# Where the second weight block of a VectorE sum is loaded: a change in the buffers of a feed-forward product

## The chip, the cores and the metric

The kernel runs on one core of a Trainium2 chip, as one program. The metric is the device time of one execution in microseconds; the time before is the median of three runs, 956.37 us (955.89 to 956.82). A profiled execution is recorded beside them, from which all rows below are taken.

## The reference

The kernel computes one layer of a hybrid decoder on 1040 rows (16 learned rows and 1024 of input) of 1024 columns: an input projection, sliding-window attention beside a gated linear recurrence, an output projection, and then a feed-forward part. The change lies in the feed-forward part, whose reference is

```
u = rmsnorm(h, g_pre_ffn[l])
f = jnp.square(jax.nn.relu(u @ w_ff1[l])) @ w_ff2[l]
h = h + rmsnorm(f, g_post_ffn[l])
```

`w_ff1` is 1024 x 4096, `w_ff2` is 4096 x 1024, all in float32.

## The kernel before

All large products are made on TensorE from float32 operands that are split in two: a high half (a cast to the rounded format, made by ScalarE at L96) and a low half (the operand less its high half, made by VectorE at L99). A product is then three matmuls: high by high (L125), high by low (L130) and low by high (L131).

Both feed-forward products are cut in two by two blocks, and made with seven block products instead of eight (Strassen's scheme). The second, `f`, is the last part of the program, from about 606 us on. `PLAN` lists its seven products `i` = 0 to 6: which blocks of the activation are added (`fx`), which blocks of `w_ff2` are added or subtracted (`wx`), and into which output quarters the product goes. Each product runs over eight slices `q` of the contracted dimension, so that there are 56 steps, numbered n = 8i + q. A step is 24 matmuls: four row tiles of 128, each with two sub-slices and three matmuls, each into its own PSUM bank.

For a step the weight sum has to be formed, cast and split. Its blocks are 128 x 1024 floats, 512 KB each:

- `fetch_2(n)` (L1258) loads the blocks. The first goes to a buffer by a load of SP's queue (L1270). The second, where the blocks are added, either is added to the first in the buffer by an accumulating transfer of GpSimd's queue (L1267, slices with `q % 3 < 2`), or is loaded to a second buffer by SP (L1270, in the slices 2 and 5).
- `prep_2(n)` (L1274) adds two blocks on VectorE where there are two (`combine`, L997: the sum goes to the first buffer), then makes the high half (ScalarE) and the low half (VectorE) into a pair of `ws` buffers, and does the same for the activation, into `b` buffers.

Steps whose sums are made by VectorE in the products 1 and 2 are (1, 2), (1, 5), (2, 2) and (2, 5), that is n = 10, 13, 18 and 21. The products 3 and 4 subtract, and take two loads in every step. The product 0 and 5 have a single block.

Buffers come from named kinds ("tags"), each with a fixed number of buffers of 4 KB or a little more in each partition. `raw` and `e` have two each, `d` has four, `ws` five, of which one holds `g_post_ffn` in this part, so that a step's pair comes free when TensorE has ended the step two before it. In the second part three of the four `d` buffers hold activations. The fourth is used in the last product by `finish_half(3)` (L1364), which loads the last rows of the residual stream for the end of the kernel (used at L1408).

Which blocks are fetched when is a loop over the steps that runs some four steps ahead. The order in which the instructions stand on each engine and in each queue is set by a scheduler at build time, by its own estimate of when buffers come free. Each queue is then worked in order: an instruction that waits holds up all behind it.

Of the kernel before, what the change touches and what calls it, by code (L numbers as in the profile page):

```python
# [37 lines left out]
def hybrid_layer(  # L38
# [19 lines left out]
    def slot(tag, shape, dt=F32):  # L58
        uid[0] += 1
        return slab.tile(shape, dt, tag=tag, name=f"{tag}{uid[0]}", bufs=bufs[tag])  # L60
# [1197 lines left out]
    def fetch_2(n):  # L1258
        i, q = steps[n]
        wx = PLAN[i][1]  # L1260
        tags = (("raw", "e"), ("e", "raw"))[n % 2] if i < 6 else LASTW[q]
        raws = []
        for (a, b), tag in zip(wx[:2], tags):
            if len(wx) == 3 and wx[2] is ADD and raws and (
                q % 3 < 2 if i < 6 else tag is None
            ):
                nc.gpsimd.dma_start(raws[0], w2v[q, a, b], accum_op=ADD)  # L1267
                break
            r = slot(tag, [P, 2, 512])
            nc.sync.dma_start(r, w2v[q, a, b])  # L1270
            raws.append(r)
        return raws
# [32 lines left out]
    for n, p in enumerate(third):  # L1305
        if n + 2 < 16:
            raw_c[third[n + 2]] = fetch_c(third[n + 2])
        if n >= 13:
            raw_2[n - 13] = fetch_2(n - 13)
        if n + 1 < 16:  # L1310
            wc[third[n + 1]] = prep_c(third[n + 1])
        if n == 15:
            gffn_b = slot("ws", [P, D])
            nc.gpsimd.dma_start(gffn_b, g_post_ffn[0].partition_broadcast(P))
            ready[0] = prep_2(0)
        if p not in a12_early:
            y2 = bank(("acc", "s")[p % 2])
            product(y2, wc[p][0], ob21, True)
            nc.vector.tensor_tensor(block("11", p), y2, block("11", p), op=ALU.add)
        y4 = bank(("pt", "o")[p % 2])  # L1320
        if n == 0:
            product_by_parts(y4, wc[p][1], ot4)
        else:
            product(y4, wc[p][1], ot4, True)
        nc.vector.tensor_tensor(block("21", p), y4, block("21", p), op=ALU.add)
        done.add(p)
        if p ^ 1 in done:
            activate("11", p // 2)
            activate("21", p // 2)
# [119 lines left out]
    for n, (i, q) in enumerate(steps):  # L1449
        while fetched < min(n + (4 if n < 45 else 6), len(steps)):  # L1450
            raw_2[fetched] = fetch_2(fetched)
            fetched += 1
        if n + 1 < len(steps):
            late = w_low[0]
            ready[n + 1] = prep_2(n + 1, "a" if n + 1 >= len(steps) - LAST else "ws")
        if q == 0:
            old = None if i == 0 else accs
            accs = [[bank(("acc", "s", "pt", "o")[j])] for j in range(4)]
            if i == 6:

                evict(5, 0, old[0][0], late)
                accs[3] = [accs[3][0][:, :256], bank("acc")[:, :256]]
        if n < len(steps) - LAST:
            for j in range(4):
                for acc, cols in zip(accs[j], col_parts(i, j)):
                    step_mm(acc, j, q, ready[n], cols)
            del ready[n]
        if old and (q > 0 or i < 6) and q < 4:
            evict(i - 1, q, old[q][0], late)
        if (i, q) in EARLY:  # L1470
            finish_early(EARLY.index((i, q)))
        if i == 6 and 1 <= q < 5:
            finish_half(q - 1)
# [36 lines left out]
```

## Time and profile before

| | |
|---|---|
| median of three runs | 956.37 us (955.89 to 956.82) |
| the profiled execution's own time | 954.71 us |
| its span, first to last instruction | 953.0 us |
| TensorE busy | 941.2 us, 99% of the span |
| VectorE, ScalarE, GpSimd busy | 658.9, 507.8, 132.1 us |
| granted clock of TensorE over the span | 0.999 |

The rows of the profile name the engines PE (TensorE), PEld (its weight loads), DVE (VectorE), ACT (ScalarE), POOL (GpSimd) and SP (SyncE); a "q" behind an engine means its queue. A timeline row gives the start in us from the start of the span, the duration, the engine, the line, the operation and the tiles (out<-in, with the buffers' kinds as names), and in brackets how long the engine sat idle before it and what ended that. "To landing" is the time from a transfer's issue until its data is there.

### The profile page before, as it was taken

How to read it: one execution, taken by the hardware profiler on the slowest of the kernel's cores; microseconds unless marked ns; L12 is line 12 of the kernel's file. 1: busy time of each engine (PE TensorE's matmuls, PEld its weight loads, DVE VectorE, ACT ScalarE, POOL GpSimd, SP SyncE). 2: the span in 40 equal slices, each digit the busy share in tenths (PEclk: the TensorE clock that was granted, in tenths of full speed). 3: DMA queues.
4: the chain of work that ended last, by engine and by line, in shares of the span. 5: the costliest groups of instructions: out<-in, count | busy, mean ns of one | idle time of the engine just before them, and what ended most of it. 6: DMA issues, size and time to landing. Idle time of an engine off the chain costs nothing.

```text
span 953.0 us, 12421 instructions
## 1 busy us (share of the span) xinstructions
PE 941.2 (99%) x4712; PEld 787.1 (83%) x4712; DVE 658.9 (69%) x849; ACT 507.8 (53%) x858; POOL 132.1 (14%) x205
## 2 busy tenths in 40 slices
PE   9999999999999999999999999999999999999997
PEld 8999999877888878888888888888888788888885
DVE  6668788879865887665644465476568576769883
ACT  8546766568645564443655575654433343445441
POOL 4104546410020100010000000001111100001201
PEclk9999999999999999999999999999999999999999
DMA  8220011104225468674422364334778765637934
GB/s 272 56 67 23 24 45 44 46 23 133 86 108 174 142 220 266 199 239 151 163 89 88 111 201 131 101 114 117 175 171 202 180 199 178 198 134 201 241 66 89
DMA packets 88199, 130.21 MB, mean 137 GB/s; under 512 B 13702, under 2 KB 52630, under 8 KB 88140
## 3 DMA queue, kind: packets, MB, share of 16 engines
q1 hardware_dynamic: 78972, 104.44, 34.4%
q0 software_dynamic: 8880, 24.19, 11.9%
q8 instruction: 37, 0.61, 0.3%
q10 hardware_dynamic: 288, 0.79, 0.2%
q14 instruction: 22, 0.18, 0.1%
HBM read 109.93 MB, written 18.87 MB: 135 GB/s over the span
## 4 chain that ended last, share of the span: by engine, by line
PE 91%; DVE 5%; ACT 2%; issue 1%; DMA 0%; DVEq 0%; SPq 0%
PE ps_acc L125 10%; PE ps_acc L131 10%; PE ps_acc L130 10%; PE ps_s L131 6%; PE ps_s L130 6%; PE ps_s L125 6%; PE ps_pt L130 6%; PE ps_pt L131 6%; PE ps_pt L125 6%; PE ps_o L131 5%; PE ps_o L130 5%; PE ps_o L125 5%; ACT c L82 1%; PE ps_o L696 1%; PE ps_acc L282 1%
## 5 line engine op out<-in xcount | busy, mean ns | idle before, releaser
L99 DVE TENSOR_TENSOR ws<-raw,ws 128x1024 fp32r<-128x1024 f32 (+1 forms) x69 | 82.6, 1197 | 71.0 <-ACT ws L96 24.1
L96 ACT CAST ws<-raw 128x1024 fp32r<-128x1024 f32 (+1 forms) x68 | 69.7, 1025 | 92.8 <-PE ps_o L130 25.0
L125 PE MATMUL ps_acc<-a,ws 128*128 128x256 f32 (+2 forms) x272 | 88.6, 326 | 0.7 <-DVE b L479 0.4
L130 PE MATMUL ps_acc<-a,ws 128*128 128x256 f32 (+2 forms) x272 | 87.9, 323 | 0.0
L96 ACT CAST ws<-e 128x1024 fp32r<-128x1024 f32 x41 | 43.0, 1050 | 83.4 <-PE ps_o L130 33.2
L131 PE MATMUL ps_acc<-a,ws 128*128 128x256 f32 (+2 forms) x272 | 87.5, 322 | 0.0
L99 DVE TENSOR_TENSOR b<-b,b 128x1024 fp32r<-128x1024 f32 (+2 forms) x50 | 58.9, 1178 | 24.7 <-PE ps_o L130 19.5
L99 DVE TENSOR_TENSOR ws<-e,ws 128x1024 fp32r<-128x1024 f32 x41 | 50.1, 1222 | 33.4 <-ACT ws L96 20.0
L96 ACT CAST b<-b 128x1024 fp32r<-128x1024 f32 (+2 forms) x49 | 50.0, 1019 | 43.6 <-DVE b L997 38.1
L683 POOL TENSOR_SCALAR_AFFINE_SELECT c<-c 128x512 fp32r<-128x512 f32 x64 | 55.5, 884 | 68.9 <-ACT c L96 54.9
L125 PEld LDWEIGHTS ps_acc<-a,ws 128*128 128x128 f32 x272 | 51.3, 188 | 5.4 <-issue 0.9
L131 PEld LDWEIGHTS ps_acc<-a,ws 128*128 128x128 f32 x272 | 51.2, 188 | 4.0 <-issue 0.2
L130 PEld LDWEIGHTS ps_acc<-a,ws 128*128 128x128 f32 x272 | 51.2, 188 | 3.7 <-issue 0.2
L125 PE MATMUL ps_acc<-ws,b 128*128 128x512 f32 (+1 forms) x120 | 46.4, 388 | 1.1 <-ACT ws L96 1.1
L130 PE MATMUL ps_acc<-ws,b 128*128 128x512 f32 (+1 forms) x120 | 46.2, 385 | 0.1
L131 PE MATMUL ps_acc<-ws,b 128*128 128x512 f32 (+1 forms) x120 | 46.2, 385 | 0.0
L125 PE MATMUL ps_pt<-ws,b 128*128 128x512 f32 x112 | 44.2, 395 | 0.0
L131 PE MATMUL ps_pt<-ws,b 128*128 128x512 f32 x112 | 44.1, 394 | 0.0
L130 PE MATMUL ps_pt<-ws,b 128*128 128x512 f32 x112 | 44.1, 393 | 0.0
L125 PE MATMUL ps_s<-ws,b 128*128 128x512 f32 x110 | 43.5, 395 | 0.0
L130 PE MATMUL ps_s<-ws,b 128*128 128x512 f32 x110 | 43.4, 394 | 0.0
L131 PE MATMUL ps_s<-ws,b 128*128 128x512 f32 x110 | 43.2, 393 | 0.0
(413 smaller groups left out, 2660.0 us busy)
## 6 DMA issues: line engine op xcount, KB each, us to landing
raw<-in_w_ff_dram SPq DMA_DIRECT2D x61, 512.0 KB, 3.5
e<-in_w_ff_dram SPq DMA_DIRECT2D x45, 512.0 KB, 4.0
a<-in_w_ff_dram SPq DMA_DIRECT2D x12, 512.0 KB, 5.5
s_dram<-a POOLq DMA_DIRECT2D x12, 512.0 KB, 3.8
raw<-in_w_in_dram SPq DMA_DIRECT2D x9, 512.0 KB, 3.8
c<-in_x_dram SPq DMA_DIRECT2D x8, 512.0 KB, 4.9
d<-in_x_dram SPq DMA_DIRECT2D x8, 512.0 KB, 4.6
out_dram<-raw SPq DMA_DIRECT2D x8, 512.0 KB
```

The source lines that it names most:

```text
L82: ins = nc.scalar.activation(*args, **kwargs).ins
L96: nc.scalar.copy(hi, src)
L99: low = nc.vector.tensor_tensor(lo, src, f32(hi), op=ALU.subtract).ins
L125: ins = nc.tensor.matmul(dst, lh, rh, start=start, stop=False, skip_group_check=True).ins
L130: nc.tensor.matmul(dst, lh, rl, start=False, stop=False, skip_group_check=True)
L131: last_mm[0] = nc.tensor.matmul(dst, ll, rh, start=False, stop=stop, skip_group_check=True).ins.name
L282: last_mm[0] = nc.tensor.matmul(acc[:, :n], w[k // 2][:, kc, :], u[kc][k % 2][:, t0 : t0 + n], start=k == 0 and kc == 0, stop=k == last an ...
L683: nc.gpsimd.affine_select(out=p_[:, :, s], in_=f32(p_[:, :, 0]), pattern=[[0, 4], [g, P]], compare_op=op, fill=0.0, base=0, channel_multip ...
L696: nc.tensor.matmul(two[:, :, oc : oc + w], v, p_.rearrange("p (j i) s c -> p j (i s c)", j=2)[:, :, pc : pc + w], start=n == 0 and k == 0, ...
```

## The change

In the steps of the products 1 and 2, the second of the two buffers is taken from the kind `d` instead of `raw` or `e`. Steps whose second block is added by the accumulating transfer take no second buffer, so only the steps 10, 13, 18 and 21 are touched.

```
         tags = (("raw", "e"), ("e", "raw"))[n % 2] if i < 6 else LASTW[q]
+        if i in (1, 2):
+            tags = tags[0], "d"
         raws = []
         for (a, b), tag in zip(wx[:2], tags):
```

The order of the built program changes with it. On TensorE and ScalarE it stays. On VectorE the sums of the steps 10, 13 and 18 move one to three places ahead, to before the low half of an earlier step; the sum of step 21 stays. On GpSimd's queue the accumulating transfers of the steps 22 and 23 change places, so that 22 comes first. On SP's queue the second blocks of the steps 10, 13, 18 and 21 come earlier: that of step 10 stands where the load of `finish_half(3)` stood, in the third part of the first feed-forward product; those of 13, 18 and 21 stand ahead of the first blocks of the steps 11, 14 and 19. The load of `finish_half(3)` stands behind the first block of step 23. The first block of step 22 stands ahead of that of step 23.

More of the change, by code (lines that the diff above doesn't have):

```diff
@@ L1261, in fetch_2 @@
         tags = (("raw", "e"), ("e", "raw"))[n % 2] if i < 6 else LASTW[q]
+        if i in (1, 2):
+            tags = tags[0], "d"
         raws = []
```

## The prediction

> **What bounds the kernel now.** I read the page first, then what TensorE waits for, then the timeline of every engine around that wait. A step is called by its number n = 8i + q (product i, block q): the four steps of the change are 10, 13, 18 and 21.
>
> ```profile
> PE 941.2 (99%) x4712; PEld 787.1 (83%) x4712; DVE 658.9 (69%) x849; ACT 507.8 (53%) x858; POOL 132.1 (14%) x205
> ...
> PE 91%; DVE 5%; ACT 2%; issue 1%; DMA 0%; DVEq 0%; SPq 0%
> ```
>
> TensorE is busy for 941.2 of 953.0 us, and the chain that ended last runs 91% over it. The number of its instructions does not change, so the change can only give or take TensorE's idle time. Of that there is one piece in the whole second feed-forward part. The waits of TensorE from 600 to 945 us show it:
>
> ```profile
> PE ps_acc L125 <- ACT ws L96: 1.1, 1, 1.1
> ```
>
> Its place, in the timeline of TensorE:
>
> ```profile
> 754.42 0.40 PE L131 MATMUL ps_o<-ws,b 128*128 128x512 f32 x1
> 755.91 0.50 PE L125 MATMUL ps_acc<-ws,b 128*128 128x512 f32 x1 [1.09 <-ACT ws L96]
> 756.25 0.39 PE L125 MATMUL ps_s<-ws,b 128*128 128x512 f32 x1
> 756.48 0.40 PE L125 MATMUL ps_pt<-ws,b 128*128 128x512 f32 x1
> 756.72 0.40 PE L125 MATMUL ps_o<-ws,b 128*128 128x512 f32 x1
> 757.17 0.50 PE L130 MATMUL ps_acc<-ws,b 128*128 128x512 f32 x1
> 757.51 0.39 PE L131 MATMUL ps_acc<-ws,b 128*128 128x512 f32 x1
> ```
>
> Starts follow each other by 0.23 us here (756.25 to 756.48). Beyond that pitch, 754.42 to 755.91 loses 1.26, 755.91 to 756.25 loses 0.11, 756.72 to 757.17 loses 0.22 and 757.17 to 757.51 loses 0.11: 1.70 us together. The boundary is that between steps 21 and 22. A step is 24 matmuls, 24 x 0.23 = 5.5 us.
>
> What was late is step 22's high half, a cast on ScalarE:
>
> ```profile
> 743.46 1.05 ACT L96 CAST ws<-e 128x1024 fp32r<-128x1024 f32 x1 [1.91 <-PE ps_o L130]
> ...
> 754.82 1.04 ACT L96 CAST ws<-raw 128x1024 fp32r<-128x1024 f32 x1 [7.79 <-PE ps_o L131]
> ```
>
> The cast at 743.46 is step 21's. Its buffer came free when TensorE ended step 19, so step 22's was due one step later, at 749.0. The row names TensorE for the 754.82, but the ws buffers that step 22 takes are those of step 20, done by 749.0. What else the cast needs is its weight sum, which POOL's queue makes by an accumulating transfer:
>
> ```profile
> 732.11 1.22 POOL L1267 DMA_DIRECT2D raw<-in_w_ff_dram  x1 [6.75 <-issue]
> 740.95 1.20 POOL L1267 DMA_DIRECT2D e<-in_w_ff_dram  x1 [7.62 <-DVE b L997]
> 748.76 1.22 POOL L1267 DMA_DIRECT2D raw<-in_w_ff_dram  x1 [6.61 <-issue]
> ```
>
> ```profile
> DMA to landing us min/median/max: 6.0/6.7/7.5
> ```
>
> The second fence is L1267's between 739 and 756 us, that is of the last two rows: 7.5 and 6.0 us. The one of 740.95 (into e, step 23) landed at about 748.45, and only 0.3 us later the one of 748.76 (into raw, step 22) went out. It landed at 748.76 + 6.0 = 754.76, just ahead of the cast. So accumulating transfers run one at a time, and step 23's stands before step 22's although it is needed later.
>
> Why step 22 is second is seen in SP's loads and the VectorE work that frees their buffers:
>
> ```profile
> 729.18 1.22 DVE L99 TENSOR_TENSOR ws<-raw,ws 128x1024 fp32r<-128x1024 f32 x1
> ...
> 734.72 1.22 DVE L99 TENSOR_TENSOR ws<-e,ws 128x1024 fp32r<-128x1024 f32 x1
> ...
> 736.46 1.21 DVE L997 TENSOR_TENSOR e<-e,raw 128x1024 f32<-128x1024 f32 x1
> ```
>
> ```profile
> 730.42 0.37 SPq L1270 DMA_DIRECT2D raw<-in_w_ff_dram  x1
> ```
>
> ```profile
> 735.97 0.37 SPq L1270 DMA_DIRECT2D e<-in_w_ff_dram  x1
> 737.70 0.37 SPq L1270 DMA_DIRECT2D raw<-in_w_ff_dram  x1
> ```
>
> Step 18's low half ends at 730.40 and frees a raw buffer, but step 21's second block takes it (730.42). Step 22's first block gets the raw that step 21's sum frees at 736.46 + 1.21 = 737.67 (737.70), after step 23's first block at 735.97.
>
> **The change part by part.** *No work is added.* Four loads of 512 KB, four sums, and all accumulating transfers stay; only buffers and places in the queues of SP, POOL and VectorE move. That costs nothing by itself.
>
> *The first of the four second blocks* (step 10) finds a d buffer free early and stands in SP's queue where the load of the last residual rows stood. That load goes behind step 23's first block and waits for step 21's sum:
>
> ```profile
> L1364 SPq DMA_DIRECT2D d<-out_dram x1: 498/498/498, 540.4 to 540.4; - x1
> ```
>
> ```profile
> L1408 DVE SCALAR_TENSOR_TENSOR a<-a,rs,d x2: 746/749/752, 947.6 to 948.2; 128x512 f32<-128x512 f32 x2
> ```
>
> From about 738 to its use at 947.6 it has 209 us: nothing. The sums of step 10 lose nothing by a block that is there 120 us early.
>
> *The other three second blocks* wait on SP for the sum before them, because one d buffer is turned over. Queued behind them are the loads of steps 11 and 12, of 14, and of 19. Before, the first of each group waited for the same sum too, since that sum freed its raw or e buffer. So SP's queue gets these no later, unless the sum itself is later: the price is nothing, and that of the exception is in the last rival.
>
> *Step 22 on POOL.* Now step 22's first block takes the raw free at 730.40, and on POOL its accumulating transfer stands ahead of step 23's (the built program has them so). The load is there by 730.42 + 5.2 = 735.6 even at the slow rate shown below. The transfer before it on POOL, at 732.11, was over by 740.95 at the latest; at 6.0 it was over by 738.1. Of all L1267 the times are these:
>
> ```profile
> DMA to landing us min/median/max: 5.6/6.0/9.3
> ```
>
> At the median step 22 lands at 738.1 + 0.3 + 6.0 = 744.4, at the worst 741.3 + 9.3 = 750.6; the cast (1.05 us) must be over by 754.65. Cover: 9.2 us, at worst 3.0. Step 23 then lands 6.3 later (750.7), at worst 9.6 later (760.2), and its cast must be over at 754.65 + 5.5 = 760.2: 8.4 us of cover, and at worst 1.0 short, which takes three extreme transfers in a row. The whole 1.70 us goes.
>
> A page of the Trainium skill would see nothing there: DMA: Bandwidth & Descriptors, Anatomy of one DMA, fits about 2.0 us plus bytes over 436 GB/s for a transfer from GpSimd's queue, an estimate of 3.2 us for 512 KB. By that step 22 would have landed at 740.95 + 3.2 + 0.3 + 3.2 = 747.7, ahead of the 749.0, and the sum would be 0. The measured 7.5 and 6.0 decide against it for transfers that also add.
>
> *What is late next.* After step 22 comes step 24's sum, which keeps its time, and then step 25's:
>
> ```profile
> 751.08 1.22 DVE L997 TENSOR_TENSOR raw<-raw,e 128x1024 f32<-128x1024 f32 x1 [0.73 <-DMA e<-in_w_ff_dram]
> ```
>
> ```profile
> 760.72 1.23 DVE L997 TENSOR_TENSOR e<-e,raw 128x1024 f32<-128x1024 f32 x1 [1.33 <-DMA raw<-in_w_ff_dram]
> ```
>
> Step 24's sum leaves step 22's low half, queued behind it on VectorE, ending at 751.08 + 1.22 + 1.22 = 753.5, before the 754.65. Step 25's raw block goes into step 22's buffer and comes earlier with it, by more than the 1.70. So TensorE stays fed, and 1.70 is carried to the end.
>
> *Sum.* The profiled execution took 954.71 us, its span 953.0: 954.71 - 1.70 = 953.0. The median of the runs shown is 956.37, 1.66 above that execution: 956.37 - 1.70 = **954.7**. The bounds of the gain: 1.70 hangs on two transfers of 7.5 + 6.0 = 13.5 us. Two of 5.6 would leave nothing to gain. This one took far longer:
>
> ```profile
> 701.58 1.22 POOL L1267 DMA_DIRECT2D e<-in_w_ff_dram  x1 [5.05 <-DVE b L997]
> ...
> 710.44 1.20 POOL L1267 DMA_DIRECT2D raw<-in_w_ff_dram  x1 [7.64 <-issue]
> ```
>
> 8.9 us from one issue to the next is 8.6 of transfer; with 6.0 behind it the two make 14.6, and the gain 2.8. If all 1.66 by which the runs exceed the profiled execution were this stall, the gain would be 3.4, and the time 953.0.
>
> **The rivals.** *The rows are right by their letter:* ScalarE's cast waited for TensorE, not for the transfer, and the change removes nothing: 956.4. For it speaks the releaser named at 754.82; against it that every other step frees its buffer two steps ahead, and that the landing falls within 0.06 us of the cast. I give it 0.10.
>
> *The sums come too early.* In the built program the sums of steps 10, 13 and 18 stand one to three places earlier on VectorE, ahead of the low halves of steps 7, 10 and 15, which TensorE wants. A sum that waits for its first block holds those up. Issue of the first block, and the casts from which the due times follow:
>
> ```profile
> 662.69 0.37 SPq L1270 DMA_DIRECT2D raw<-in_w_ff_dram  x1
> ```
>
> ```profile
> 680.36 0.37 SPq L1270 DMA_DIRECT2D e<-in_w_ff_dram  x1
> ```
>
> ```profile
> 708.18 0.37 SPq L1270 DMA_DIRECT2D raw<-in_w_ff_dram  x1
> ```
>
> ```profile
> 671.27 1.05 ACT L96 CAST ws<-raw 128x1024 fp32r<-128x1024 f32 x1 [4.53 <-PE ps_o L130]
> ...
> 687.91 1.05 ACT L96 CAST ws<-e 128x1024 fp32r<-128x1024 f32 x1 [1.01 <-PE ps_o L130]
> ...
> 710.20 1.05 ACT L96 CAST ws<-e 128x1024 fp32r<-128x1024 f32 x1 [2.05 <-PE ps_o L130]
> ```
>
> The cast at 671.27 marks the start of step 7, that at 687.91 of step 10, and step 15 starts at 710.20 + 5.5 = 715.7. TensorE first uses low halves after four matmuls, 0.9 later: 672.2, 688.8, 716.6. Sum and low half take 2.4. So the loads may take 672.2 - 2.4 - 662.7 = 7.1, 6.0 and 6.0 us. What they take, beside an accumulating transfer:
>
> ```profile
> 689.85 1.23 DVE L997 TENSOR_TENSOR e<-e,raw 128x1024 f32<-128x1024 f32 x1 [4.07 <-DMA raw<-in_w_ff_dram]
> ```
>
> ```profile
> 684.68 0.37 SPq L1270 DMA_DIRECT2D raw<-in_w_ff_dram  x1
> ```
>
> ```profile
> DMA to landing us min/median/max: 3.2/3.6/7.6
> ```
>
> That load took 5.2 us, under 6.0 by 0.8; the median of L1270 is 3.6, the longest 7.6. At 7.6 the three stalls are 0.5 + 1.6 + 1.6 = 3.7, against the 1.70: +2.0, 958.4. It turns slower above 6.9 us (twice 0.85 over). The loads do move closer to the accumulating transfers, so I give it 0.18. In the Trainium skill, DMA: Bandwidth & Descriptors, Issuing engines are not separate DMA queues, has transfers of all queues share the same 16 engines and interleave, and so speaks against the change in this place; the 5.2 against 3.6 agrees.
>
> **How the numbers follow.** Stall removed 0.72, nothing removed 0.10, sums too early 0.18. The bound of 0.2% is 1.9 us, about what a measurement of this kernel can tell from no change, and 1.70 lies just inside it. Of the 0.72 I put 0.42 beyond (the runs are longer than the profiled execution, and 0.2 us more of stall is enough) and 0.30 within. So faster 0.42, same 0.40, slower 0.18. The range reaches from 953.0 (gain 3.4) to the last rival's 958.4.
>
> **What would show it.** Right: no wait of TensorE on ScalarE near 755; two POOL transfers in a row into raw and e there in that order, raw first, landed before 750; SP's residual load near 738. Wrong: TensorE idle before low halves near 672, 689 or 716 with VectorE's sum just ahead; or the gap at 754.4 unchanged, with the cast starting although the transfer had long landed.

## The result and the profile after

The changed kernel takes 953.29 us (median of seven runs, 953.15 to 953.75), the kernel before 956.37 (seven runs, 954.32 to 958.12). The ratio is 0.9966, with an interval of 0.9953 to 0.9980: faster by 0.34%, or 3.1 us. The runs also lie closer together, 0.6 us from end to end for 3.8. The profiled execution of the changed kernel took 953.59 us, its span 951.9.

TensorE works as long as before (941.2 us), so what is gone is idle time:

```profile
PE 941.2 (99%) x4712; PEld 787.7 (83%) x4712; DVE 659.2 (69%) x849; ACT 508.2 (53%) x858; POOL 131.4 (14%) x205
```

The boundary of the steps 21 and 22 in TensorE's timeline, the place of the 1.70 us:

```profile
754.58 0.40 PE L130 MATMUL ps_o<-ws,b 128*128 128x512 f32 x1
754.82 0.40 PE L131 MATMUL ps_o<-ws,b 128*128 128x512 f32 x1
755.06 0.39 PE L125 MATMUL ps_acc<-ws,b 128*128 128x512 f32 x1
755.29 0.39 PE L125 MATMUL ps_s<-ws,b 128*128 128x512 f32 x1
```

The starts follow each other by 0.23 to 0.24 us straight through. From 600 to 945 us the list of TensorE's waits is empty. Step 22's cast, the second of these rows of ScalarE's timeline, and the accumulating transfers on POOL (two lines were added to the kernel, so that L1267 and L1270 are now L1269 and L1272):

```profile
743.86 1.05 ACT L96 CAST ws<-e 128x1024 fp32r<-128x1024 f32 x1 [1.91 <-PE ps_o L130]
...
749.45 1.06 ACT L96 CAST ws<-raw 128x1024 fp32r<-128x1024 f32 x1 [2.02 <-PE ps_o L130]
...
755.02 1.05 ACT L96 CAST ws<-e 128x1024 fp32r<-128x1024 f32 x1 [3.57 <-PE ps_o L130]
```

```profile
734.96 1.20 POOL L1269 DMA_DIRECT2D raw<-in_w_ff_dram  x1 [6.56 <-DMA raw<-in_w_ff_dram]
742.62 1.22 POOL L1269 DMA_DIRECT2D e<-in_w_ff_dram  x1 [6.47 <-DVE ws L99]
```

Step 22 (raw) now goes out at 734.96 instead of 748.76, ahead of step 23 (e). Its cast starts at 749.45, when its buffer comes free, and no longer at 754.82. The loads on SP in this stretch:

```profile
736.37 0.37 SPq L1272 DMA_DIRECT2D e<-in_w_ff_dram  x1
738.10 0.34 SPq L1366 DMA_DIRECT2D d<-out_dram  x1
```

Step 22's first block is not among them any more (it went out at 730.82). The residual load (into d) stands where the prediction put it.

In the accounts below, the stall of an execution is the sum of what TensorE loses between 600 and 930 us. It is worked out from TensorE's timeline: each distance of two starts above 0.29 us counts, less the pitch of 0.23. Ratios are to the kernel before on the same chip, with a 95% interval in brackets.

### The profile page after: what moved, and what is told of

It is laid out like the page before. It is cut to its first block, busy times and chain, and to the rows that moved or that the text cites. A ratio compares the mean times of both kernels' runs of the same rounds, so it can differ in the third digit from the quotient of the medians.

```text
span 951.9 us, 12417 instructions
## 1 busy us (share of the span) xinstructions
PE 941.2 (99%) x4712; PEld 787.7 (83%) x4712; DVE 659.2 (69%) x849; ACT 508.2 (53%) x858; POOL 131.4 (14%) x205
## 4 chain that ended last, share of the span: by engine, by line
PE 86%; DVE 7%; ACT 3%; issue 2%; DMA 2%; SPq 0%; DVEq 0%; POOL 0%; ACTq 0%
PE ps_acc L125 10%; PE ps_acc L131 10%; PE ps_acc L130 10%; PE ps_s L131 6%; PE ps_s L125 6%; PE ps_s L130 6%; PE ps_pt L130 6%; PE ps_pt L131 6%; PE ps_pt L125 6%; PE ps_o L131 5%; PE ps_o L130 5%; PE ps_o L125 5%; ACT c L82 1%; PE ps_o L696 1%; PE ps_acc L282 1%
```

## The experiments

Theory A: step 22 waited for its accumulating transfer because step 23's stood before it. Theory B: the gain comes from the freed `raw` and `e` buffers, by which all loads are earlier. All four kernels of the first set ran on one chip, beside a kernel before with a median of 956.84 us (29 runs, 953.47 to 958.53).

**Step 21 alone.**

```
-        if i in (1, 2):
+        if n == 21:
             tags = tags[0], "d"
```

(on the changed kernel, as is the next)

> Only step 21 takes its second block into a d buffer; steps 10, 13 and 18 stay as before. The built program then has step 22's accumulating transfer ahead of step 23's, and nothing else of weight is moved. Theory A (the order of steps 22 and 23 on GpSimd's queue is the whole cost): the idle time of TensorE at 754 us is gone, about 953.3 us, all of the 3.1 gained. Theory B (the gain comes from three more free buffers, which make all loads of products 1 and 2 earlier): about a quarter of the gain, 955.6 us, and idle time is left near 754.

Measured: 953.61 us (953.01 to 954.36), ratio 0.9970 (0.9959 to 0.9981). One of the four buffers gives all of the gain that can be told apart. Its profile has no stall near 754, and one of 0.31 us at 722.

**The other three alone.**

```
-        if i in (1, 2):
+        if n in (10, 13, 18):
             tags = tags[0], "d"
```

> Steps 10, 13 and 18 take d buffers, step 21 does not; step 23's accumulating transfer stays ahead of step 22's. Theory A: 956.4 us within the spread of before (954.3 to 958.1), with 1 to 4 us of idle time on TensorE at 754. Theory B: about 954.0 us, three quarters of the gain.

Measured: 954.00 us (952.93 to 954.50), ratio 0.9971 (0.9962 to 0.9981). That is theory B's number: here step 23 still stands ahead of step 22, and the gain came all the same. Of the stall at 755, 0.26 us is left. Theory A as stated fell with it: the order is not the only way to the gain.

**The order alone.**

```
+    adds = {}
...
-                nc.gpsimd.dma_start(raws[0], w2v[q, a, b], accum_op=ADD)
+                adds[n] = nc.gpsimd.dma_start(raws[0], w2v[q, a, b], accum_op=ADD).ins
+                if n == 23:
+                    behind(adds[22].name, adds[23])
```

(on the kernel before; `behind(x, y)` makes y stand behind x)

> All buffers as before, but step 23's accumulating transfer is made to stand behind step 22's on GpSimd's queue. Step 22's load is issued at 737.7 as before and lands by about 741.5, so its accumulating transfer runs from about 742 to 748, step 23's to 754 or 756. Theory A: no idle time at 754, about 953.3 us. Theory B: no gain, 956.4 us.

Measured: 953.21 us (952.78 to 955.08), ratio 0.9969 (0.9959 to 0.9979). All buffers are those of before, and the gain is whole. Theory B as stated fell too. Its profile has no stall at 754, and 0.45 us at 694.7, of which more below.

**All four buffers, with the old order.**

```
...
+                if n == 23:
+                    behind(adds[23].name, adds[22])
```

(on the changed kernel; `adds` is filled as in the edit above)

> All four d buffers as in the changed kernel, but step 22's accumulating transfer is made to stand behind step 23's again. Step 23's load lands at about 741, its accumulating transfer at 748, step 22's at 754. Theory A: the idle time at 754 is back, 1 to 4 us, about 956.4 us. Theory B: 953.3 us.

Measured: 953.82 us (952.98 to 954.52), ratio 0.9972 (0.9961 to 0.9982). The stall at 754 is back with 0.90 us in the profile, which is less than any of the kernel before shown below.

So the buffers alone and the order alone are each enough, and the two do not add. What they share is that step 22's transfer lands earlier, as POOL shows. The kernel with the three buffers and the old order:

```profile
739.98 1.20 POOL L1269 DMA_DIRECT2D e<-in_w_ff_dram  x1 [11.82 <-DMA e<-in_w_ff_dram]
745.93 1.22 POOL L1269 DMA_DIRECT2D raw<-in_w_ff_dram  x1 [4.75 <-DVE b L997]
```

Step 23's transfer starts 1 us earlier than before (740.95), and it took less. The earlier start fits with step 23's load (issued at 735.89 here, 735.97 before): it no longer overlaps step 20's accumulating transfer, which runs from 726.9 to 733.0 here and ran from 732.1 to 737.8 before. The time from issue to landing of step 23's transfer, here and then in the kernel before:

```profile
DMA to landing us min/median/max: 5.6/5.6/5.6
```

```profile
DMA to landing us min/median/max: 7.5/7.5/7.5
```

Together that lands step 22's 2.0 us sooner (752.7 for 754.7), where the profile of before had lost 1.70. Why 5.6 and not 7.5 was not tried by itself; the rows suggest that it is the load of step 24, which follows the issue by 0.6 us before and by 1.5 us here (SP's load into raw at 741.57 and 741.50). The other traces agree. Twelve of the profiles of this study have the descriptor room of before (an edit below changes it), and each has twelve accumulating transfers between 650 and 760 us. With a load of SP issued up to 1.0 us behind them, 27 of 28 took over 7.0 us; of the 116 others 19 did, and their median is 5.8. Of these 19, 14 have a load issued 0.03 to 0.28 us ahead of them instead.

**Other executions of the kernel before.** What stayed open was the size: 3.1 us gained, 1.70 seen. Three more executions of the unchanged kernel were profiled. Rival D: the spread of before has nothing to do with this place.

> The kernel before, unchanged, for another profiled execution. Theory A as it stands after the first four runs (what varies is only how late step 22's accumulating transfer lands, by whether loads are issued within about 1 us of an accumulating transfer and stretch it from 5.6 to 6.0 us to 7 to 8.7): TensorE loses 0 to 5 us at the boundary of steps 21 and 22, and the execution's own time less all stalls of TensorE in the second feed-forward part is 953.0 to 954.0. Rival D (the spread of before is something else, for example the input stage or the tail): stalls of about 1.7 us in each, whatever the time.

> As the run before it: a third profiled execution of the kernel before. Theory A: time less stalls in the second feed-forward part is 953.0 to 954.0 us; rival D: it varies with the time.

> As the run before it: a fourth profiled execution of the kernel before. Theory A: time less stalls in the second feed-forward part is 953.0 to 954.0 us; rival D: it varies with the time.

Measured, with the profiles of the changed kernel and of the first four edits beside them:

| execution | own time, us | stall, us | time less stall |
|---|---|---|---|
| before (the prediction's) | 954.71 | 1.70 | 953.0 |
| before, second | 955.79 | 2.37 | 953.4 |
| before, third | 957.01 | 3.80 | 953.2 |
| before, fourth | 956.83 | 3.26 | 953.6 |
| changed | 953.59 | 0 | 953.6 |
| step 21 alone | 953.95 | 0.31 | 953.6 |
| the other three | 953.43 | 0.26 | 953.2 |
| order alone | 954.11 | 0.45 | 953.7 |
| four buffers, old order | 954.12 | 0.90 | 953.2 |

The time less the stall is 953.0 to 953.7 in all nine: rival D fell. (The five kernels further below give 952.4 to 953.3.) Before, the stall is 1.70 to 3.80, with a mean of 2.8, and the profile that the prediction read was the mildest of the four. In each of the four, step 23's transfer took 7.3 to 7.5 us, with step 24's load 0.4 to 0.6 us behind its issue. The third execution names the transfer itself as what ended ScalarE's wait:

```profile
755.65 1.04 ACT L96 CAST ws<-raw 128x1024 fp32r<-128x1024 f32 x1 [8.64 <-DMA raw<-in_w_ff_dram]
```

In its timeline of TensorE the stall is not only the gap:

```profile
754.40 0.40 PE L131 MATMUL ps_o<-ws,b 128*128 128x512 f32 x1
756.75 0.77 PE L125 MATMUL ps_acc<-ws,b 128*128 128x512 f32 x1 [1.94 <-ACT ws L96]
757.31 0.63 PE L125 MATMUL ps_s<-ws,b 128*128 128x512 f32 x1
757.74 0.63 PE L125 MATMUL ps_pt<-ws,b 128*128 128x512 f32 x1
758.16 0.63 PE L125 MATMUL ps_o<-ws,b 128*128 128x512 f32 x1
```

The gap is 2.35 - 0.23 = 2.12 us; then the matmuls start 0.43 us apart instead of 0.23, which makes up the other 1.68. The three other executions lose 0.44 to 0.45 behind their gaps too, so some 1.2 of the 1.68 is particular to this one. The stretches of that execution show why (the columns are the stretch and its length, the busy time of PE, PEld, DVE, ACT and POOL with the number of instructions, then the granted clock, the busy share of the DMA engines and their GB/s):

```profile
754.00:757.00 3.00, 1.06 (x5) 0.57 (x4) 0.28 (x1) 1.35 (x2) 0.00 (x0) 0.97 0.85 240
757.00:760.00 3.00, 3.00 (x8) 2.35 (x9) 3.00 (x3) 2.54 (x3) 0.00 (x0) 0.50 0.28 88
760.00:765.00 5.00, 5.00 (x23) 4.06 (x22) 2.58 (x3) 1.04 (x2) 0.00 (x0) 0.98 0.74 230
```

The granted clock fell to 0.50 for about 3 us. It was not the only such execution, as far as the mean clock tells: of the 81 executions of before that were timed beside the runs of this study, the 14 with the lowest mean granted clock (0.996, as the third execution) took 957.1 to 958.5 us, the 67 others had a median of 955.3.

The fourth execution has a second stall, 1.0 of its 3.26 us, at 694.5:

```profile
694.53 0.40 PE L125 MATMUL ps_o<-ws,b 128*128 128x512 f32 x1
695.64 0.50 PE L130 MATMUL ps_acc<-ws,b 128*128 128x512 f32 x1 [0.71 <-DVE ws L99]
```

There TensorE waited for the low half of step 11. In VectorE's timeline it stands behind step 13's sum, which waited for its second block:

```profile
692.09 1.22 DVE L997 TENSOR_TENSOR e<-e,raw 128x1024 f32<-128x1024 f32 x1 [6.00 <-DMA raw<-in_w_ff_dram]
693.23 1.22 DVE L997 TENSOR_TENSOR b<-a,b 128x1024 f32<-128x1024 f32 x1
694.37 1.22 DVE L99 TENSOR_TENSOR ws<-e,ws 128x1024 fp32r<-128x1024 f32 x1
```

With the d buffer of the changed kernel that block no longer comes last: SP issues it at 667.84, and step 13's sum waits for its first block until 683.73. The 0.45 us at 694.7 with the order alone is the same stall.

**Twice the room for GpSimd's descriptors.** Why does step 22's transfer wait for step 23's at all? This edit doubles the setting for the room that the descriptors of GpSimd's transfers have. The small column tiles get two buffers instead of four, to make place for it.

```
-    small = ctx.enter_context(tc.tile_pool(name="small", bufs=4))
+    small = ctx.enter_context(tc.tile_pool(name="small", bufs=2))
...
-        "TRN2", target_bir_lowering=False, num_devices=1, dynamic_dma_scratch_size=1024
+        "TRN2", target_bir_lowering=False, num_devices=1, dynamic_dma_scratch_size=2048
```

(on the kernel before)

> The kernel before with twice the space for GpSimd's transfer descriptors (2048 for 1024; for the room the tiny column tiles get 2 buffers instead of 4). The order on every engine is that of before, step 23's accumulating transfer still stands ahead of step 22's. Theory A with the reading that one transfer fills the descriptor space: the next accumulating transfer goes out before the one ahead has landed, step 22's at about 742 to 743, and TensorE's stall at 754 is gone: 953.3 us. Rival (they run one at a time for another reason): issues stay 0.3 us behind the landing ahead, stall and 956.8 us stay.

Measured: 952.91 us (952.25 to 953.63), ratio 0.9967 (0.9956 to 0.9977), no stall. The order of instructions on every engine is that of the kernel before. POOL's timeline:

```profile
739.16 1.20 POOL L1267 DMA_DIRECT2D e<-in_w_ff_dram  x1 [13.27 <-DMA e<-in_w_ff_dram]
741.82 1.20 POOL L1267 DMA_DIRECT2D raw<-in_w_ff_dram  x1 [1.46 <-DMA raw<-in_w_ff_dram]
```

Step 22's transfer goes out 2.7 us after step 23's, as soon as its own load is there, with step 23's still under way. The tiles' part of the edit, alone on the kernel before:

> The kernel before with two buffers instead of four for the tiny column tiles and the descriptor space as before: the other half of the edit of the run with the doubled space. The order on all engines is that of before. If the doubled space alone removed the stall: transfers run one at a time again, stall of 1.5 to 4 us at 754, about 955.6 us (the 1.0 us gained ahead of 108 us stays, if it comes from these tiles). If the column tiles did it: 952.9 us.

Measured: 956.32 us (954.37 to 957.83), ratio 1.0007 (0.9995 to 1.0019) to a kernel before with a median of 955.22 (35 runs) on that chip: nothing gained. Its profile (957.83 us, the slowest of its twelve executions) has a stall of 4.69 us, and on POOL the transfers go one at a time again:

```profile
742.43 1.20 POOL L1267 DMA_DIRECT2D e<-in_w_ff_dram  x1 [7.64 <-DMA e<-in_w_ff_dram]
750.22 1.22 POOL L1267 DMA_DIRECT2D raw<-in_w_ff_dram  x1 [6.59 <-issue]
```

So it was the descriptor room that made the accumulating transfers go one at a time. This is the third way to the same gain.

**A longer wait.** One more transfer, between the two:

```
+    spare, adds = dpool.tile([P, 2, 512], F32, name="spare"), {}
...
+                if n == 22:
+                    adds["x"] = nc.gpsimd.dma_start(spare, w2v[q, a, b]).ins
...
+                if n == 23:
+                    behind(adds[23].name, adds["x"])
+                    behind(adds["x"].name, adds[22])
```

(on the kernel before)

> The kernel before with one more transfer of 512 KB on GpSimd's queue (a block of the weights to a scratch tensor, used by nothing), between step 23's and step 22's accumulating transfers; all else stands as before. Theory A (what TensorE waits for at 754 is how late step 22's transfer lands): it lands about one transfer later, 4 to 6 us, the idle time there grows from 1.7 to 3.8 us to about 6 to 9, and, if an idle stretch of over 2 us brings the granted clock to 0.5 for some 3 us as in one of the looks at before, about 1.7 more: 960 to 963 us. Rival D (the letter of the row: the cast waits for TensorE): no change, 956.6 us.

Measured: 957.33 us (953.92 to 960.25), ratio 1.0016 (0.9998 to 1.0033): not the 960 to 963 that theory A expected, and not a clear loss. The profiled execution is the fastest of the ten (953.92 us), with a stall of 0.81 us; what the longer ones lost was not profiled. POOL's timeline shows that the edit did not do what it was for:

```profile
740.19 1.20 POOL L1271 DMA_DIRECT2D e<-in_w_ff_dram  x1 [9.44 <-DVE b L99]
740.90 1.22 POOL L1270 DMA_DIRECT2D spare<-in_w_ff_dram  x1
746.37 1.20 POOL L1271 DMA_DIRECT2D raw<-in_w_ff_dram  x1 [4.25 <-DVE b L997]
```

The plain transfer to a scratch tensor went out right behind step 23's, beside it, and step 22's went out 0.3 us after the landing of step 23's (740.19 + 5.9), without waiting for the plain one, which landed at 748.2. It seems to have fitted the descriptor room where a second accumulating one did not; that was not tried by itself. As a test of the size this run says nothing.

**Together.** The changed kernel with the tiles' edit, and with both edits:

> The changed kernel with two buffers for the tiny column tiles. Theory A: no stall in the second feed-forward part in either, so only what these tiles bring ahead of 108 us: 952.3 us if it is 1.0, 953.3 if nothing.

> The changed kernel with the doubled descriptor space (and two buffers for the tiny column tiles). Theory A: with no stall left for it to remove, the doubled space brings nothing over the run before it: 952.3 us, within 0.5.

Measured: 953.25 us (952.34 to 955.58) and 953.47 (952.87 to 955.31), both with a ratio of 0.9977 (0.9965 to 0.9989 and 0.9966 to 0.9989). With next to no stall left, more room brings nothing, as expected. The 1.0 us expected from the tiles ahead of 108 us did not show in the times. The profiled spans are shorter (951.0 and 950.9 us, for 951.9 of the changed kernel), but some 0.6 us more of the time lies outside the span. No version here is clear of the changed kernel. On this chip the kernel before took 955.22, so that the gain is 2.0 and 1.8 us: its size differs from one set of runs to the next.

## Why the prediction was right, and where it was short

*The stall, its place and its cause* held. The gap at 754.4 is gone, the cast waits for its buffer, step 22's transfer stands first and landed at 734.96 + 5.7 = 740.7, earlier than the 744.4 forecast: step 20's transfer ahead of it, which the prediction left at 732.11, went out at 727.18. The rival that the row is right by its letter fell: the same row of another execution names the transfer.

*"The whole 1.70 us goes"* held: none of it is left in the profile. The two profiled executions differ by 1.1 us only (954.71 and 953.59), since without the stall they take 953.0 and 953.6, the spread that the table shows. As the gain of the runs the term was mis-sized: 1.70 forecast, 3.1 measured. The forecast of 954.7 lies 1.4 above the 953.29. The step that was short is "the bounds of the gain": it took one execution's stall as the likeliest and left the 1.66 us by which the median exceeded it as a bound. Four executions give 1.70 to 3.80, mean 2.8. Two of the reasons were not in the sum at all: the halved clock after the gap (some 1.2 us in the third execution) and the second stall at 694 (1.0 us in the fourth). That 953.29 lies inside the range, near its end of 953.0, is owed to that bound: it counted the 1.66 as more of the same stall, which the four profiles bear out on the whole. The spread of the runs of before was a sign that the stall varied; with it gone the spread fell from 3.8 us to 0.6. That is not the whole of the spread everywhere: the changed kernel with the tiles' edit, without a stall in its profile, spread over 3.2 us.

*That "only buffers and places in the queues" move* named three things, of which one, POOL's order, was made the cause. The runs show a cause with more than one end: the order alone gives the gain, and so do three of the buffers without the order, and so does more descriptor room without either. The prediction's claim that the first three buffers cost nothing was right, that they bring nothing (it gave them no term) was not: alone they bring 2.8 us.

*The sums too early* did not cost in the changed kernel. The loads took 3.5 us (663.09 to the sum at 666.59), 4.0 (679.75 to 683.73) and at most 4.5 (708.58 to 713.03), against the 7.1, 6.0 and 6.0 allowed. The mechanism showed once, where the prediction put it: 0.30 us at 715.6 in the profile with both edits, with step 18's sum just ahead of step 15's low half. Step 18's first block was issued there at 707.32, beside two accumulating transfers (705.34 and 706.81), and its sum began 6.3 us later, over the 6.0 allowed:

```profile
713.61 1.23 DVE L997 TENSOR_TENSOR raw<-raw,d 128x1024 f32<-128x1024 f32 x1 [1.89 <-issue]
714.76 1.22 DVE L99 TENSOR_TENSOR ws<-e,ws 128x1024 fp32r<-128x1024 f32 x1
```

## What to carry to other kernels

A short stall of a bound engine that hangs on two transfers in a row differs from execution to execution: read its size from several profiles, or from the spread of the runs, before it becomes a term of a sum. Where accumulating transfers go one at a time, their order in the queue is part of the schedule, and so is the room for their descriptors. Before a gain is put down to one of several things that moved, do each alone: here three different edits, of the buffers, of the order and of the descriptor room, each gave the whole of it.

## What the runs showed of the hardware

After a gap of 2.1 us, TensorE's granted clock was 0.50 for about 3 us in the third execution of before (1.68 us lost beside the gap), and likewise after 2.2 us in the profile with the two tile buffers; after gaps of 1.9 and 1.8 us in the second and fourth execution it stayed at 1.00. In the Trainium skill, TensorE: Matmul & The Clock Gate, What's actually happening, the clock halves after an idle window of about 3.4 us; here 2.1 us were enough. In the profile with the two tile buffers TensorE had worked for 1 us again, from 757.2, before the clock fell:

```profile
756.00:758.00 2.00, 0.84 (x4) 0.67 (x4) 0.86 (x1) 1.93 (x3) 0.00 (x0) 1.00 0.29 111
758.00:760.00 2.00, 1.96 (x6) 1.29 (x5) 2.00 (x3) 1.95 (x3) 0.00 (x0) 0.55 0.24 77
760.00:762.00 2.00, 2.00 (x7) 1.57 (x6) 0.97 (x2) 0.00 (x0) 0.00 (x0) 0.60 0.61 214
```

With the setting of 1024 for the descriptor room, an accumulating transfer of 512 KB went out only when the one ahead had landed, 0.31 us later or more in all 132 pairs of the twelve profiles; with 2048, two were under way together (issued at 739.16 and 741.82, the first landing at 744.8).

An accumulating transfer of 512 KB took 5.6 to 6.0 us from issue to landing in most cases, and over 7.0 in 27 of 28 where SP issued a load of 512 KB up to 1.0 us behind it.
